# Two z blocks as plain products in place of four, and token sums by DMA

## The chip, the cores and the metric

The kernel runs on one core of a Trainium2 chip. The metric is the device time of one execution in microseconds (us). Each engine has a queue of its own and works it off in order: TensorE (PE) multiplies, VectorE (DVE) and ScalarE (ACT) work elementwise, GpSimd (POOL) here issues DMAs and does a few small operations, SyncE (SP) issues DMAs. An instruction starts when its turn has come and the semaphores that it waits for are there.

## The reference

One layer of a hybrid encoder block on 512 tokens and 16 meta tokens (528 columns), D = 2048:

```python
h = rms_norm(x, norm_g)
proj = h @ w_in                      # 2048 x 12368
(q_a, k_a, v_a, z_a, q_i, k_i, w_i, q_b, f_b, i_b, z_b, gates) = jnp.split(proj, cuts, axis=-1)
...
score = jnp.einsum('bqhs,bqh->bqs', jax.nn.relu(idx_logits), wib)   # token indexer, 16 heads
_, sel = lax.top_k(score, topk)
...
y_b = o_b.reshape(B, T, BRANCH_WIDTH) * jax.nn.silu(z_b)
...
merged = jnp.sum(g * p, axis=2)
return x + merged @ w_out
```

The change concerns `h @ w_in`, and there the columns of `z_b`, which are eight blocks of 128.

## The kernel before

Every fp32 operand is held as a high and a low part (names ending in H and L, or wh and wl for weights), and each product is three matmuls: high by high, high by low, low by high. The token matrix h is kept turned, in 16 row blocks hH[k], hL[k] of 128 x 528 (two halves of 264 columns).

The columns of w_in are computed in two ways. A plain job (`Job`) takes one block of 128 columns: 16 row blocks x 3 matmuls of 512 columns into one PSUM tile pg. A pair (`Pair`, `run_pair`) takes two blocks of 128 columns by a scheme with seven products instead of eight: 7 x 8 x 3 matmuls of 256 columns. The seven are listed in `SEVEN` (L1317): each names a weight operand (`11`, `s2`, `12`, `s3`, `s1`, `22`, `s4`, of which s1 to s4 are sums of weight chunks) and a token operand (`11`, `t2`, `21`, `t3`, `t1`, `t4`, `22`). A weight operand is split by ScalarE (wh) and VectorE (wl) just ahead of its product; three buffers of each stand in turn. The sums s1 and s2 are made on VectorE, s3 and s4 by an adding DMA from GpSimd's queue (L118).

The token operands t1 to t4 are made once, for row blocks k = 0 to 7 with their partners 8 + k, by two tasks of `tops_task` (L1272), which run beside the plain jobs. For one k: r1 = hH[k] + hL[k] and r2 of the partner (two VectorE operations of 528 columns, tiles tr), differences of their halves, and the splits (tiles tT). t3 is kept aside as a float32 tile and put over the right half of hH[k], hL[k] by `place_t3` (L1305), as soon as no plain job needs that half.

Before the change the order is: the key and index blocks (1 + 8 plain jobs), z blocks 0 to 3 as plain jobs (NZ = 4), then 40 pairs, and after them the branch and output products. Beside the plain jobs run the index tasks: for each head pair the queries are turned and split (tiles qst, from qxc), multiplied with the split keys (kkH, kkL) on TensorE into small tiles psc, passed through ScalarE's relu (rl), and added up on VectorE (score). After the last head the search of the 128 largest (`topk_task`) runs on VectorE.

The order of the instructions is set when the program is built. A planner (class `Core`) keeps a clock for each engine with costs that are written in it, and `pump` lets a task add its next instructions when its time has come by these clocks. An instruction that the planner puts early in a queue still waits on the chip for what it reads. Tiles come from 69 equal buffers (`Slots`); a new tile takes the free one whose last use is the oldest by the planner's clocks, and its first writer waits for that last use.

Of the kernel before, what the change touches and what calls it, by code (L numbers as in the profile page):

```python
# [8 lines left out]
F32 = mybir.dt.float32  # L9
F32R = mybir.dt.float32r  # L10
BF16 = mybir.dt.bfloat16
U8 = mybir.dt.uint8
AF = mybir.ActivationFunctionType
OP = mybir.AluOpType
# [16 lines left out]
WAIT = object()  # L31
# [7 lines left out]
ROOM = 2  # L39
SAME = {"pe": 0.0, "act": 60.0, "dve": 125.0, "pool": 60.0}  # L40
MARGIN = 300.0
NSLOT = 69
NZ = 4


class Core:
# [70 lines left out]
    def dma_add(self, out, a):  # L117
        self.nc.gpsimd.dma_start(out, a, accum_op=OP.add)  # L118
        return self.at("pool", 4000.0, [out], [out, a])

    def ts(self, out, a, s1, s2, op0, op1=None):
        if op1 is None:
            self.nc.vector.tensor_scalar(out, a, s1, None, op0=op0)
        else:
            self.nc.vector.tensor_scalar(out, a, s1, s2, op0=op0, op1=op1)
        ins = [a] + [s for s in (s1, s2) if s is not None and not isinstance(s, (int, float))]
        return self.at("dve", 65 + 0.53 * self.n(out), [out], ins)
# [57 lines left out]
def hybrid_kernel(ctx, tc, x, meta, vecs, w_in, rows, w_branch, w_out,  # L185
# [7 lines left out]
    E = Core(nc)  # L193
    S = Slots(E, sp, [f"s{i}" for i in range(NSLOT)], [128, T], None)
# [4 lines left out]
    tasks, hold = [], []  # L199
# [39 lines left out]
    def finish(t):  # L239
        while not t.done:  # L240
            pump(1e9)
            if t.done:
                break
            nxt = [u for u in tasks if u.t > E.clk["pe"]]
            if nxt:
                E.clk["pe"] = max(E.clk["pe"], min(u.t for u in nxt))
            else:
                assert any(u.step() for u in list(tasks)), "stuck"
# [13 lines left out]
    def slots(name, n=1, dt=F32):  # L262
        return [S.get(name, dt) for _ in range(n)]

    def slot(name, dt=F32):
        return S.get(name, dt)
# [238 lines left out]
    hH, hL = [], []  # L505
# [113 lines left out]
    idx_left = [8]  # L619
# [646 lines left out]
    TB = {}  # L1266

    def tops_task(i):


        lo, hi, al = slice(0, 264), slice(264, 528), slice(0, 528)
        for k in range(4 * i, 4 * i + 4):  # L1272
            while len(S.free) < (8 + ROOM if idx_left[0] else 6) or k > 3 and k - 4 not in TB:
                yield WAIT
            if k % 2 == 0:
                t3 = slot("t3")
            r1, r2, t1, c = slots("tr", 4)
            d = t3[:, 264 * (k % 2):264 * (k % 2) + 264]
            E.tt(r1[:, al], hH[k][:, al].bitcast(F32), hL[k][:, al].bitcast(F32), OP.add)
            yield E.tt(r2[:, al], hH[8 + k][:, al].bitcast(F32), hL[8 + k][:, al].bitcast(F32), OP.add)  # L1280
            E.tt(t1[:, lo], r1[:, lo], r1[:, hi], OP.subtract)
            E.tt(t1[:, hi], t1[:, lo], r2[:, hi], OP.add)
            E.tt(d, r1[:, hi], r2[:, hi], OP.subtract)
            e = E.tt(c[:, lo], r2[:, lo], t1[:, hi], OP.subtract)
            S.put(r1, r2)
            yield e
            a, b, t4 = slots("tT", 3, F32R)
            E.act(a[:, al], t1[:, al], AF.Copy)
            E.act(t4[:, lo], c[:, lo], AF.Copy)
            E.tt(b[:, al], t1[:, al], a[:, al].bitcast(F32), OP.subtract)  # L1290
            e = E.tt(t4[:, hi], c[:, lo], t4[:, lo].bitcast(F32), OP.subtract)
            S.put(t1, c)
            TB[k] = {"11": (hH[k][:, lo], hL[k][:, lo]), "t3": (hH[k][:, hi], hL[k][:, hi]),
                     "21": (hH[8 + k][:, lo], hL[8 + k][:, lo]), "22": (hH[8 + k][:, hi], hL[8 + k][:, hi]),
                     "t1": (a[:, lo], b[:, lo]), "t2": (a[:, hi], b[:, hi]), "t4": (t4[:, lo], t4[:, hi]),
                     "tiles": (a, b, t4), "t3f": d, "t3s": t3}
            yield e

    def place_t3(k0):
        for k in range(k0, k0 + 4):  # L1300
            h, l = TB[k]["t3"]
            E.act(h, TB[k]["t3f"], AF.Copy)
            E.tt(l, TB[k]["t3f"], h.bitcast(F32), OP.subtract)
            if k % 2:
                S.put(TB[k]["t3s"])  # L1305
# [13 lines left out]
    def run_pair(pr, nxt, late, last):  # L1319

        w = pr.w
        bk, W, V = {}, slice(0, w), slice(w, 2 * w)
        for i, (wn, tn, bn, on_) in enumerate(SEVEN):
            op = pr.ops[i]
            split_upto(op["prep"] + 2)
            if not on_:
                bk[bn] = B1.get("p" + bn)
            b = bk[bn][:, W]
            for k in range(8):
                th, tl = (t[:, 264 - w:264] for t in TB[k][tn])  # L1330
                st_ = k == 0 and not on_
                E.mm(b, op["h"][k], th, st_, False, loose=True)
                E.mm(b, op["h"][k], tl, False, False, loose=True)
                E.mm(b, op["l"][k], th, False, k == 7, loose=True)
                pump()
            if i == 0:
                p1 = main_slot("p1")
            elif i == 1:
                E.tt(p1[:, V], p1[:, W], b, OP.subtract)
            elif i == 3:  # L1340
                E.tt(p1[:, W], b, p1[:, W], OP.subtract)
                B1.put(bk["y"])
            elif i == 4:
                g2 = main_slot("g2")
                E.tt(g2[:, V], p1[:, W], b, OP.subtract)
            elif i == 5:
                E.tt(g2[:, W], p1[:, W], b, OP.add)
                B1.put(bk["w"])
            elif i == 6:
                E.tt(g1[:, V], p1[:, V], b, OP.add)  # L1350
                B1.put(bk["z"])
                S.put(p1)
            if i == 1:
                sum_4(pr)
            if i > 2 and i < 6 and nxt:
                (sum_1, sum_2, sum_3)[i - 3](nxt)
            split_upto(op["prep"] + 3)
            if i == 0:
                E.act(p1[:, W], b, AF.Copy)
            if late:  # L1360
                late.pop(0)()
            if i == 2:
                g1 = main_slot("g1")
                E.act(g1[:, W], b, pr.f)
                B1.put(bk["x"])
            elif i == 5:
                late.append(lambda g=g2: pr.done[1](g))
            elif i == 6:
                late.append(lambda g=g1: pr.done[0](g))
            if last:  # L1370
                if i == 1:
                    while len(y_out) < 8:
                        pump(1e9)
                        if len(y_out) < 8:
                            E.clk["pe"] += 200
                    yr = load_y(0, 4, nc.scalar)
                elif i == 3:
                    S.put(*hH[:8], *hL[:8])
                    yr += load_y(4, 8, nc.gpsimd)
                    ysplit = split_y(yr, 1)  # L1380
                elif i == 4:
                    S.put(*[t for k in range(8) for t in TB[k]["tiles"][:2]])
                elif i == 5:
                    S.put(*[TB[k]["tiles"][2] for k in range(8)])
                elif i == 6:
                    S.put(*hH[8:], *hL[8:])
                    late.pop(0)()
                    load_gates(1, 0)
                if i in (4, 5):
                    for _ in range(4):  # L1390
                        next(ysplit, None)
# [174 lines left out]
    t_task = []  # L1566

    def pre_t():
        t_task.extend(spawn(tops_task(i), 2) for i in range(2))
# [10 lines left out]
    jobs += [Job("in", C_QI + 128 * j, 128, done=d_qi(j)) for j in range(8)]  # L1580
    jobs += [Job("in", C_ZB + 128 * h, 128, done=d_zb(h)) for h in range(NZ)]
    jobs[3].pre = pre_t
# [15 lines left out]

    for h in range(NZ, 8, 2):
        two(Z[h], Z[h + 1])  # L1600
# [69 lines left out]
    for half in range(2):  # L1670
        n = (272, 256)[half]
        for kt in range(KT):
            prep_next()
            for ji in range(2):
                if ji == 0:
                    c = slice(272 * half, 272 * half + n)
                    o = kb[:80, half, :n]
                else:
                    c = slice(8 + 264 * half, 264 + 264 * half)
# [13 lines left out]
    npair, late, ahead = 0, [], []  # L1693
    first_out = min(i for i, j in enumerate(jobs) if j.kind == "out")
    for ji, job in enumerate(jobs[2:], 3):
# [5 lines left out]
        if job.kind == "pair":  # L1701
            npair += 1
            if npair == 1:
                for t in t_task:
                    finish(t)
                place_t3(0)
                place_t3(4)
                late += [lambda: None, lambda: hold.clear()]
            last = npair == len(pairs)
            run_pair(job, None if last else jobs[ji], late, last)  # L1710
            continue
        if job.kind == "out":
# [4 lines left out]
            nxt = jobs[ji] if ji < len(jobs) else None  # L1717
# [6 lines left out]
        if job.meta:  # L1724
            b = [B1.get("pg"), B1.get("pg")]
            parts = [(b[c][:, :264], slice(264 * c, 264 * c + 264)) for c in range(2)]
        else:
            b = B1.get("pg")
# [104 lines left out]
```

## Time and profile before

| what | us |
|---|---|
| three runs | 1515.77, 1517.16, 1517.38 (median 1517.16) |
| profiled execution, its own time | 1516.59 |
| span of its instructions | 1514.8 |
| TensorE, VectorE, ScalarE, GpSimd busy | 1498.3, 1176.8, 679.3, 199.8 |
| plain jobs | 51.4 to 197.06 |
| last index product ends | 166.14 |
| first pair | 197.06 to 216.91 |

A profile row gives the start, the time and the shape of an instruction or a group; a bracket at its end gives how long the engine had been idle and what ended that. TensorE's granted clock is 1.00 in every stretch. Matmuls overlap, so what one costs is the distance of two starts, not its own time.

### The profile page before, as it was taken

The numbers are of one execution on the slowest core, as the hardware profiler recorded it, in microseconds if no ns is written. First come the engines' busy times: TensorE is split into PE (matmuls) and PEld (weight loads), VectorE is DVE, ScalarE is ACT, GpSimd is POOL, SyncE is SP. The second block draws the span as 40 slices with busy tenths as digits, with TensorE's granted clock in tenths as the row PEclk, the third lists the DMA queues.
The fourth block names the chain that finished last, engine by engine and source line by source line (L and its number), as shares of the span: only waits on it lengthen the run. The fifth ranks groups of instructions, "written<-read, shape, count | busy, mean of one in ns | idle before, by whom it ended". The sixth has DMA issues, their size and how long they took to land.

```text
span 1514.8 us, 30989 instructions
## 1 busy us (share of the span) xinstructions
PE 1498.3 (99%) x12648; PEld 1418.5 (94%) x12648; DVE 1176.8 (78%) x1971; ACT 679.3 (45%) x1048; POOL 199.8 (13%) x241
## 2 busy tenths in 40 slices
PE   7999999999999999999999999999999999999998
PEld 6888899999999999999999999999998888889998
DVE  6699999999998778678868786886665565878775
ACT  5555444444444433443344334434456662334332
POOL 3100000001111100000010000000032110102222
PEclk9999999999999999999999999999999999999999
DMA  9222368776877765675666657666798444548773
GB/s 268 84 70 70 104 147 190 186 182 166 219 200 197 187 156 134 168 168 134 168 162 149 157 138 176 158 143 167 181 271 283 146 132 125 155 136 213 215 213 85
DMA packets 300959, 250.08 MB, mean 165 GB/s; under 512 B 12932, under 2 KB 267920, under 8 KB 300816
## 3 DMA queue, kind: packets, MB, share of 16 engines
q1 hardware_dynamic: 274080, 167.95, 37.9%
q0 software_dynamic: 20656, 72.81, 24.5%
q10 hardware_dynamic: 6080, 7.34, 1.4%
q8 instruction: 99, 1.62, 0.4%
q14 instruction: 44, 0.36, 0.1%
HBM read 168.00 MB, written 27.62 MB: 129 GB/s over the span
## 4 chain that ended last, share of the span: by engine, by line
PE 97%; ACT 1%; issue 1%; DVE 0%; DMA 0%; POOL 0%; ACTq 0%; DVEq 0%; POOLq 0%
PE pg L94 21%; PE pz L92 16%; PE py L92 16%; PE px L92 16%; PE po L92 10%; PE pw L92 8%; PE phl L94 2%; PE psc L94 1%; PE pov L92 1%; PE plg L94 1%; PE pho L94 1%; PE ppt L98 1%; PE phs L94 1%; PE px L98 1%; PE pqa L98 0%
## 5 line engine op out<-in xcount | busy, mean ns | idle before, releaser
L102 ACT ACTIVATE wh<-raw 128x1024 fp32r<-128x1024 f32 x304 | 322.1, 1061 | 509.0 <-PE pz L92 129.4
L109 DVE TENSOR_TENSOR wl<-raw,wh 128x1024 fp32r<-128x1024 f32 x302 | 372.7, 1235 | 133.4 <-ACT wh L102 132.0
L92 PE MATMUL px<-hH,wh 128*128 128x256 f32 (+1 forms) x672 | 193.7, 288 | 0.0
L92 PE MATMUL px<-hH,wl 128*128 128x256 f32 (+1 forms) x672 | 189.5, 282 | 0.0
L92 PE MATMUL px<-hL,wh 128*128 128x256 f32 (+1 forms) x672 | 189.4, 282 | 0.0
L102 ACT ACTIVATE wh<-sum 128x1024 fp32r<-128x1024 f32 x100 | 106.1, 1061 | 180.3 <-PE pw L92 72.5
L92 PE MATMUL po<-wh,mh 128*128 128x256 f32 x896 | 158.6, 280 | 0.5 <-DVE xq L109 0.5
L109 DVE TENSOR_TENSOR wl<-sum,wh 128x1024 fp32r<-128x1024 f32 x100 | 127.1, 1271 | 34.8 <-ACT wh L102 34.6
L92 PEld LDWEIGHTS po<-wh,mh 128*128 128x128 f32 x896 | 137.5, 189 | 0.8 <-DVE xq L109 0.7
L92 PEld LDWEIGHTS px<-hH,wh 128*128 128x128 f32 x672 | 126.6, 188 | 0.9
L92 PEld LDWEIGHTS px<-hH,wl 128*128 128x128 f32 x672 | 126.6, 188 | 0.0
L92 PEld LDWEIGHTS px<-hL,wh 128*128 128x128 f32 x672 | 126.4, 188 | 0.0
L92 PE MATMUL po<-wl,mh 128*128 128x256 f32 x448 | 125.8, 281 | 0.0
L92 PE MATMUL py<-tT,wh 128*128 128x256 f32 (+1 forms) x672 | 124.7, 285 | 0.0
L92 PE MATMUL pw<-tT,wh 128*128 128x256 f32 (+1 forms) x672 | 124.6, 285 | 0.0
L92 PE MATMUL pz<-tT,wh 128*128 128x256 f32 (+1 forms) x672 | 123.6, 284 | 0.0
L118 POOL DMA_DIRECT2D raw<-raw x50 | 43.2, 863 | 518.4 <-DVE sum L109 518.4
L92 PEld LDWEIGHTS py<-tT,wh 128*128 128x128 f32 x672 | 103.4, 189 | 0.5
L92 PEld LDWEIGHTS pw<-tT,wh 128*128 128x128 f32 x672 | 103.2, 189 | 0.2
L92 PEld LDWEIGHTS pz<-tT,wh 128*128 128x128 f32 x672 | 103.2, 188 | 0.2
L94 PE MATMUL pg<-yH,wh 128*128 128x512 f32 x256 | 102.9, 402 | 0.0
L94 PE MATMUL pg<-yL,wh 128*128 128x512 f32 x256 | 100.9, 394 | 0.0
(317 smaller groups left out, 3797.0 us busy)
## 6 DMA issues: line engine op xcount, KB each, us to landing
raw<-in_w_in_dram SPq DMA_DIRECT2D x192, 512.0 KB, 4.6
raw<-raw POOLq DMA_DIRECT2D x50, 512.0 KB, 5.3
raw<-sum POOLq DMA_DIRECT2D x50, 512.0 KB, 5.4
raw<-in_w_branch_dram SPq DMA_DIRECT2D x32, 512.0 KB, 5.2
raw<-in_w_out_dram SPq DMA_DIRECT2D x32, 512.0 KB, 3.9
gd<-g SPq DMA_DIRECT2D x32, 256.0 KB, 5.0
g<-gd POOLq DMA_DIRECT2D x30, 256.0 KB, 3.4
x<-in_x_dram SPq DMA_DIRECT2D x16, 256.0 KB, 5.5
```

Source lines behind the costliest of these rows:

```text
L92: self.nc.tensor.matmul(out, lhsT, rhs, start=start, stop=stop, skip_group_check=True)
L94: self.nc.tensor.matmul(out, lhsT, rhs, start=start, stop=stop)
L98: self.nc.tensor.transpose(out, in_, ident)
L102: self.nc.scalar.activation(out, in_, f, **kw)
L109: self.nc.vector.tensor_tensor(out, a, b, op=op)
L118: self.nc.gpsimd.dma_start(out, a, accum_op=OP.add)
```

## The change

```diff
-NZ = 4
+NZ = 2
...
+    def dma(self, out, a, op=None):
+        if op is None:
+            self.nc.gpsimd.dma_start(out, a)
+        else:
+            self.nc.gpsimd.dma_start(out, a, accum_op=op)
+        t = max([self.clk["pool"]] + [self.wr.get(x.tensor.name, (0.0,))[0] for x in (a, out)])
+        self.clk["pool"] = max(self.clk["pool"], t) + 600.0
+        e = t + 3500.0
...
+        def fetch(k):
+            r = slots("tr", 2)
+            for t, q in zip(r, (k, 8 + k)):
+                E.dma(t[:, al], hH[q][:, al].bitcast(F32))
+            for t, q in zip(r, (k, 8 + k)):
+                e = E.dma(t[:, al], hL[q][:, al].bitcast(F32), OP.add)
+            return r, e
...
-            r1, r2, t1, c = slots("tr", 4)
+            a, b, t4 = slots("tT", 3, F32R)
+            if k % 4 < 3 and len(S.free) >= (6 + ROOM if idx_left[0] else 6):
+                nxt = fetch(k + 1)
             d = t3[:, 264 * (k % 2):264 * (k % 2) + 264]
-            E.tt(r1[:, al], hH[k][:, al].bitcast(F32), hL[k][:, al].bitcast(F32), OP.add)
-            yield E.tt(r2[:, al], hH[8 + k][:, al].bitcast(F32), hL[8 + k][:, al].bitcast(F32), OP.add)
-            E.tt(t1[:, lo], r1[:, lo], r1[:, hi], OP.subtract)
-            E.tt(t1[:, hi], t1[:, lo], r2[:, hi], OP.add)
+            E.tt(r1[:, lo], r1[:, lo], r1[:, hi], OP.subtract)
             E.tt(d, r1[:, hi], r2[:, hi], OP.subtract)
-            e = E.tt(c[:, lo], r2[:, lo], t1[:, hi], OP.subtract)
+            E.tt(r2[:, hi], r1[:, lo], r2[:, hi], OP.add)
+            e = E.tt(r2[:, lo], r2[:, lo], r2[:, hi], OP.subtract)
...
@@ run_pair
+            if i == 1:
+                while t_task:
+                    finish(t_task.pop(0))
             for k in range(8):
-                th, tl = (t[:, 264 - w:264] for t in TB[k][tn])
+                th, tl = (t[:, 264 - w:264] for t in (TB[k][tn] if i else (hH[k], hL[k])))
...
@@ before the first pair
-                for t in t_task:
-                    finish(t)
-                place_t3(0)
-                place_t3(4)
-                late += [lambda: None, lambda: hold.clear()]
+                late += [lambda: None, lambda: (place_t3(0), place_t3(4)), lambda: hold.clear()]
```

Two z blocks go from plain jobs to one more pair (41 pairs). r1 and r2 are made in place: a DMA from GpSimd's queue copies the high part, a second adds the low part, 2 + 2 DMAs for each k, 32 in all; the next k is fetched while one is worked on, if buffers are free. The differences are written over r1 and r2, so two tiles fewer are held, and the split of 528 columns becomes two of 264. The first pair begins with its first product while the last row blocks' token operands are still to be made; they are finished in the build order ahead of the second product, and t3 is placed behind the second.

GpSimd's queue had, before, nothing between the key norm and the first adding DMA of a pair; rows of its order there, with the semaphores that each row waits for:

```order
L573 MEMSET kiy_829 128x320 [waits PE_49]
L113 TENSOR_TENSOR kis_830<-kis_830,mhalf 128x5 [waits DVE_49,PE_49]
L118 DMA raw_1840<-raw_1789 128x1024 [waits DMAHW2_49,DMAHW3_49,DMAHW1_49,DMAHW4_49,DVE_49,DMAHW6_49,Activation_49,Pool_49]
L118 DMA raw_2016<-sum_26_2155 128x1024 [waits DMAHW5_49,DMAHW0_49,DMAHW6_49,DVE_49,Pool_49]
L118 DMA raw_2107<-raw_2065 128x1024 [waits DMAHW6_49,DMAHW0_49,DVE_49]
```

Now the 32 DMAs stand between; here those of row block 3 (tr_1355 and its partner tr_1356; hH_361 is hH[3], hH_503 is hH[11]) with the two ahead of them:

```order
L125 DMA tr_1086<-hL_347 128x528 [waits DMASW6_49,DMASW0_49]
L125 DMA tr_1087<-hL_488 128x528 [waits DMASW7_49,DMASW1_49]
L123 DMA tr_1355<-hH_361 128x528 [waits DMASW1_49,DVE_49]
L123 DMA tr_1356<-hH_503 128x528 [waits DVE_49]
L125 DMA tr_1355<-hL_362 128x528 [waits DMASW4_49,DMASW2_49]
L125 DMA tr_1356<-hL_504 128x528 [waits DMASW5_49,DMASW3_49]
```

The copies wait for VectorE (the former user of the buffer), the adds for the copies, and the first adding DMA of a pair now stands behind all of them, right after the last row block's (7):

```order
L125 DMA tr_2019<-hL_556 128x528 [waits DMASW5_49,DMASW3_49]
L123 DMA tr_2028<-hH_438 128x528 [waits PE_49]
L123 DMA tr_2029<-hH_569 128x528 [waits DMAHW4_49,DMAHW0_49,DVE_49]
L125 DMA tr_2028<-hL_439 128x528 [waits DMASW6_49,DMASW0_49]
L125 DMA tr_2029<-hL_570 128x528 [waits DMASW7_49,DMASW1_49]
L118 DMA raw_1626<-raw_1540 128x1024 [waits DMAHW5_49,DMAHW2_49,DMAHW6_49,DMAHW0_49,Pool_49]
```

Row block 7's partner tile waits for VectorE too. On VectorE, between the last tT of row block 2 (tT_1231, which reads the buffer that tr_1355 takes) and the first operation on tr_1355 stands:

```order
L109 TENSOR_TENSOR tT_1231<-tr_1087,tT_1231 128x264
L145 SCALAR_TENSOR_TENSOR score_975<-rl_1293,tabs_98,score_975 128x272
L109 TENSOR_TENSOR tT_1098<-tr_1045,tT_1097 128x264
L109 TENSOR_TENSOR tT_1098<-tr_1046,tT_1097 128x264
L109 TENSOR_TENSOR tT_1099<-tr_1046,tT_1099 128x264
L109 TENSOR_TENSOR wl_1306<-raw_858,wh_1305 128x1024
L145 SCALAR_TENSOR_TENSOR score_976<-rl_1320,tabs_98,score_976 128x400
L109 TENSOR_TENSOR qst_1328<-qxc_1261,qst_1328 64x512
L109 TENSOR_TENSOR qst_1329<-qxc_1261,qst_1329 64x512
L145 SCALAR_TENSOR_TENSOR score_977<-rl_1340,tabs_98,score_977 128x528
L145 SCALAR_TENSOR_TENSOR score_974<-rl_1349,tabs_98,score_974 128x144
L109 TENSOR_TENSOR tr_1355<-tr_1355 128x264
```

Before, a row block's sums stood in VectorE's queue themselves and could not be late for it; the like stretch there:

```order
L109 TENSOR_TENSOR tT_1263<-tr_1108,tT_1262 128x528
L109 TENSOR_TENSOR tT_1264<-tr_1109,tT_1264 128x264
L109 TENSOR_TENSOR wl_1273<-raw_858,wh_1272 128x1024
L130 SCALAR_TENSOR_TENSOR score_983<-rl_1287,tabs_98,score_983 128x400
L109 TENSOR_TENSOR tT_1296<-tr_1046,tT_1295 128x528
L109 TENSOR_TENSOR tT_1297<-tr_1047,tT_1297 128x264
L130 SCALAR_TENSOR_TENSOR score_984<-rl_1305,tabs_98,score_984 128x528
L130 SCALAR_TENSOR_TENSOR score_981<-rl_1314,tabs_98,score_981 128x144
L109 TENSOR_TENSOR qst_1320<-qxc_1239,qst_1320 64x512
L109 TENSOR_TENSOR qst_1321<-qxc_1239,qst_1321 64x512
L130 SCALAR_TENSOR_TENSOR score_982<-rl_1332,tabs_98,score_982 128x272
L109 TENSOR_TENSOR tr_1339<-hH_346,hL_347 128x528
```

The third place is TensorE's queue at the first index products (psc_985 before, psc_978 now), in the third plain job; a piece of the difference:

```order
+L94 MATMUL psc_978<-kkH_962,qst_875 128x144
+L94 MATMUL psc_978<-kkL_963,qst_875 128x144
 L94 MATMUL pg_904<-hH_503,wh_854 128x512
 L94 MATMUL pg_904<-hL_504,wh_854 128x512
 L94 MATMUL pg_904<-hH_503,wl_855 128x512
+L94 MATMUL psc_1007<-kkH_962,qst_875 128x272
+L94 MATMUL psc_1007<-kkL_963,qst_875 128x272
 L94 MATMUL pg_904<-hH_522,wh_854 128x512
 L94 MATMUL pg_904<-hL_523,wh_854 128x512
 L94 MATMUL pg_904<-hH_522,wl_855 128x512
-L94 MATMUL psc_985<-kkH_969,qst_875 128x144
-L94 MATMUL psc_985<-kkL_970,qst_875 128x144
```

The first index product moved ahead of six plain ones.

More of the change, by code (lines that the diff above doesn't have):

```diff
@@ L119, in dma_add @@
         return self.at("pool", 4000.0, [out], [out, a])
+    def dma(self, out, a, op=None):
[6 more added lines that the diff above has]
+        e = t + 3500.0
+        for x in (a, out):
+            w = self.ac.get(x.tensor.name)
+            if not w or w[0] < e:
+                self.ac[x.tensor.name] = (e, "dma")
+        self.wr[out.tensor.name] = (e, "dma")
+        return e
     def ts(self, out, a, s1, s2, op0, op1=None):
@@ L1271, in tops_task @@
         lo, hi, al = slice(0, 264), slice(264, 528), slice(0, 528)
-        for k in range(4 * i, 4 * i + 4):
-            while len(S.free) < (8 + ROOM if idx_left[0] else 6) or k > 3 and k - 4 not in TB:
+        def fetch(k):
[5 more added lines that the diff above has]
+            return r, e
+        nxt = None
+        for k in range(4 * i, 4 * i + 4):
+            while k > 3 and k - 4 not in TB:
+                yield WAIT
+            while not nxt and len(S.free) < (6 + ROOM if idx_left[0] else 6):
+                yield WAIT
+            (r1, r2), e = nxt or fetch(k)
+            nxt = None
+            yield e
+            while len(S.free) < (4 + ROOM if idx_left[0] else 4):
                 yield WAIT
@@ L1276, in tops_task @@
                 t3 = slot("t3")
-            r1, r2, t1, c = slots("tr", 4)
+            a, b, t4 = slots("tT", 3, F32R)
+            if k % 4 < 3 and len(S.free) >= (6 + ROOM if idx_left[0] else 6):
+                nxt = fetch(k + 1)
             d = t3[:, 264 * (k % 2):264 * (k % 2) + 264]
-            E.tt(r1[:, al], hH[k][:, al].bitcast(F32), hL[k][:, al].bitcast(F32), OP.add)
-            yield E.tt(r2[:, al], hH[8 + k][:, al].bitcast(F32), hL[8 + k][:, al].bitcast(F32), OP.add)
-            E.tt(t1[:, lo], r1[:, lo], r1[:, hi], OP.subtract)
-            E.tt(t1[:, hi], t1[:, lo], r2[:, hi], OP.add)
+            E.tt(r1[:, lo], r1[:, lo], r1[:, hi], OP.subtract)
             E.tt(d, r1[:, hi], r2[:, hi], OP.subtract)
-            e = E.tt(c[:, lo], r2[:, lo], t1[:, hi], OP.subtract)
-            S.put(r1, r2)
[L1286 to L1292, printed above, removed]
+            E.tt(r2[:, hi], r1[:, lo], r2[:, hi], OP.add)
+            e = E.tt(r2[:, lo], r2[:, lo], r2[:, hi], OP.subtract)
+            yield e
+            E.act(a[:, lo], r1[:, lo], AF.Copy)
+            E.act(a[:, hi], r2[:, hi], AF.Copy)
+            E.act(t4[:, lo], r2[:, lo], AF.Copy)
+            E.tt(b[:, lo], r1[:, lo], a[:, lo].bitcast(F32), OP.subtract)
+            E.tt(b[:, hi], r2[:, hi], a[:, hi].bitcast(F32), OP.subtract)
+            e = E.tt(t4[:, hi], r2[:, lo], t4[:, lo].bitcast(F32), OP.subtract)
+            S.put(r1, r2)
             TB[k] = {"11": (hH[k][:, lo], hL[k][:, lo]), "t3": (hH[k][:, hi], hL[k][:, hi]),
```

## The prediction

> **What bounds the kernel now.** I read the page first (busy shares, then the chain that ended last), then the waits of TensorE over the whole span, then that chain in order of time where the edits stand.
>
> ```profile
> span 1514.8 us, 30989 instructions
> PE 97%; ACT 1%; issue 1%; DVE 0%; DMA 0%; POOL 0%; ACTq 0%; DVEq 0%; POOLq 0%
> PE pc L98 <- DMA vrow<-in_vecs_dram: 8.2, 1, 8.2
> PE phl L98 <- ACT wh L102: 1.1, 1, 1.1
> PE phs L94 <- ACT MT L102: 1.0, 5, 0.2
> PE pg L94 <- POOL el L113: 0.8, 1, 0.8
> ```
>
> TensorE carries 97% of the chain. It waits 8.2 us once at the start and then hardly at all: the largest later wait is 1.1 us. So only two things move the end: how long TensorE's own work is, and every microsecond for which it is newly made to wait.
>
> ```profile
> 166.14 30.91 PE pg L94 x132
> 197.06 2.85 PE px L92 x24
> ...
> 214.09 2.83 PE pz L92 x24
> 216.91 2.84 PE px L92 x24
> 80.00:100.00 20.00, 20.00 (x100) 16.88 (x99) 19.77 (x39) 10.81 (x21) 0.00 (x0) 1.00 0.29 80
> ```
>
> At 166.14 the last index product is over and 132 plain products run without a gap; the first pair takes 197.06 to 216.91. The last row is a stretch of the plain jobs in the windows view: the fourth busy figure says VectorE is busy for 19.77 of 20 us (and GpSimd for 0). VectorE is nearly full beside a TensorE that doesn't yet wait for it.
>
> **The change, part by part. Plain blocks.** A plain product costs 30.91 / 132 = 0.234 us, and a block has 48: two blocks are 96 x 0.234 = 22.48 us. In their place stands one pair more, 216.91 - 197.06 = 19.85 us. TensorE's own work falls by **2.63 us**. That is the ceiling of the gain: nothing else on TensorE gets shorter. The split of four weight chunks on ScalarE and VectorE goes and seven operands' splits and two sums come; they lie beside the extra pair as in every pair now. The order of TensorE's last 6976 rows, some two thirds, is unchanged, so I add nothing for the later phases.
>
> A rule stands against the row here. The Trainium skill, "TensorE: Matmul & The Clock Gate", section "Back-to-back issue gap", gives a gap of N / 2.4 + 2.5 ns; by it the products take 215.8 and 109.2 ns and the gain would be 2.37 us. The trace has 234 and 118 ns at a granted clock of 1.00, so it doesn't agree, and the rows decide.
>
> **First index product.** The eight row blocks' two 528-wide sums leave VectorE.
>
> ```profile
> 69.25 1.32 DVE L109 TENSOR_TENSOR tr<-hH,hL 128x528 f32<-128x528 f32 x2
> 70.49 1.22 DVE L109 TENSOR_TENSOR wl<-raw,wh 128x1024 fp32r<-128x1024 f32 x1
> 71.63 0.43 DVE L109 TENSOR_TENSOR kkL<-pki,kkH 128x272 fp32r<-128x272 f32 x1
> 72.51 0.42 DVE L109 TENSOR_TENSOR kkL<-pki,kkH 128x256 fp32r<-128x256 f32 x1 [0.45 <-ACT kkH L102]
> 68.62 1.06 ACT L102 ACTIVATE wh<-raw 128x1024 fp32r<-128x1024 f32 x1 [3.10 <-PE pg L94]
> 72.09 0.39 ACT L102 ACTIVATE kkH<-pki 128x256 fp32r<-128x256 f32 x1 [2.10 <-DVE kkL L109]
> 72.89 0.23 PE L94 MATMUL psc<-kkH,qst 128*128 128x144 f32 x1
> 72.96 0.27 PE L94 MATMUL psc<-kkL,qst 128*128 128x144 f32 x1
> ```
>
> A pair of sums takes 70.49 - 69.25 = 1.24 us. The planner therefore puts the first index product six plain products (6 x 0.234 = 1.4 us) earlier, at 71.49. But kkL comes only 0.7 us earlier: wl is held by its wh on ScalarE until 69.7 (68.62 + 1.06), so wl runs 69.7 to 70.9, the first kkL to 71.3, kkH (0.39) to 71.7, the second kkL (0.42) to 72.2. The kkL product, due at 71.56, waits until 72.2. Stall **0.6 us**; bounds 0 (if the planner's order happens to fit) and 1.4 (kkL no earlier than now).
>
> **Fetches.** Each row block now needs two copies and two adding DMAs from GpSimd's queue, 32 in all.
>
> ```profile
> L118 POOL DMA_DIRECT2D raw<-raw x50: 842/854/934, 189.3 to 1483.2; - x50
> DMA to landing us min/median/max: 4.5/5.4/8.0
> DMA to landing us min/median/max: 2.2/3.5/15.8
> g<-gd POOLq DMA_DIRECT2D x30, 256.0 KB, 3.4
> kv<-kd POOLq DMA_DIRECT2D x8, 264.0 KB, 7.2
> ```
>
> GpSimd is idle here, so 32 x 0.85 us of issuing costs nothing; what counts is latency. No 264 KB add is in the trace. A plain transfer of that size has 3.4 (g) to 7.2 us (kv, in a crowded stretch); an add of twice the size has 4.5 to 8.0, median 5.4. I take 3.4 for the copy and 4.2 for the add, nearest to the quiet rows: 7.6 us from the release of the buffer to the landed sum, some 0.8 more if both halves are late; ends 6.5 (2.2, the fastest among the transfers of g, and 4.3) and 13 (5.8 and 7.2). The planner counts 3.5 for each of the two and doesn't look at when the buffer is free. Most fetches are early. Two are not.
>
> Row block 3 (tr_1355) gets the buffer that the fetch before leaves after its last tT. Between that and its first use VectorE has this work:
>
> ```profile
> 100.14 1.04 DVE L109 TENSOR_TENSOR tT<-tr,tT 128x528 fp32r<-128x528 f32 x2
> 102.79 1.04 DVE L109 TENSOR_TENSOR tT<-tr,tT 128x528 fp32r<-128x528 f32 x2
> 106.68 0.70 DVE L109 TENSOR_TENSOR tr<-hH,hL 128x528 f32<-128x528 f32 x1
> 115.86 1.41 DVE L109 TENSOR_TENSOR qst<-qxc,qst 64x512 fp32r<-64x512 f32 x2
> 118.22 0.23 PE L94 MATMUL psc<-kkH,qst 128*128 128x144 f32 x1
> ```
>
> The stretch 100.14 to 106.68 has the same operations with one tT pair (0.96 us) more, so 5.6 us. VectorE then stands for 8.4 - 5.6 = 2.8 us, and what is queued behind is two weight splits, scores and the next head's qst. In before that qst half is done at 116.6 and TensorE takes it at 118.22: 1.6 us of slack, 2.3 with the first stall. Stall **0.5 us**; bounds 0 (landed within 7.9 us of the release) and 5 (fetch 13). Row block 5 waits in the same way, but its head's products come some 6 us after, so it is covered.
>
> **First pair.** It begins where the plain work ends, at 166.14 + 36 x 0.234 = 174.57 (before: 197.06, less the two blocks), with row block 7 and t3 missing.
>
> ```profile
> 163.32 0.69 DVE L109 TENSOR_TENSOR hz<-pg,hz 128x512 f32<-128x512 f32 x1 [1.27 <-ACT hz L102]
> 198.33 2.83 DVE L109 TENSOR_TENSOR hL<-t,hH 128x264 fp32r<-128x264 f32 x8
> ```
>
> The last fetch waits for VectorE's score of 272 columns. From hz at 163.3 come hz (0.6), two sums and a split (3 x 1.2) and that score (0.4): 167.9. Sum landed: 167.9 + 7.6 + 0.1 = 175.6; VectorE would reach it at 173.2. After it: three 264-wide operations (0.35 each, 2.83 / 8), hz 0.6, wl 1.14, two tT: 179.1. TensorE reaches that operand, the last eighth of the second product, at 174.57 + 2.84 + 2.48 = 179.9: 0.8 us to spare. The eight t3 pieces follow the second product's end (180.25): ScalarE's 1.06, wl 1.14, then 0.35 each, last at 185.4; needed from 183.1 to 185.6: 0.2 us to spare. So no wait by the sum, and each later microsecond is one of waiting. I take **0.3 us**; bounds 0 and 5.
>
> Sum: -2.63 + 0.6 + 0.5 + 0.3 = **-1.2 us**. The profiled execution took 1516.59 us (span 1514.8 and 1.8 around it); the median shown is 1517.16, 0.6 higher, runs 1515.77 to 1517.38. Prediction **1515.4 us**. A difference of 0.2%, 3.0 us, is about what a measurement can tell from no change; the ceiling of the gain is 2.63, so it is "no change" unless a stall goes wrong.
>
> The Trainium skill, "DMA: Bandwidth & Descriptors", section "Anatomy of one DMA — SWDGE (gpsimd) path", gives 2.0 us plus bytes / 436 GB/s: 2.6 us for each transfer here and 5.2 for a fetch. By that rule both fetch stalls vanish (a rival below). For the 512 KB add it would give 3.2, where the rows have 5.4: the trace doesn't agree, and I don't use it.
>
> **Rivals.** *Clean*: fetches and kkL are on time, the full 2.63 us: 1514.0. For it: no row of TensorE shows a wait now though VectorE is as full. Against: the kkL arithmetic.
> *Fetches in time*: at the low end, 6.5 us, row block 3 is held for 6.5 + 0.8 - 5.6 = 1.7 us, inside its slack, and the first pair gains a microsecond; kkL alone remains: -2.63 + 0.6, 1514.6. Against: 2.2 us is the fastest of 30 rows.
> *Cancelled*: each stall is 1 us larger: -2.63 + 4.4, 1518.4. For it: slacks of 0.2 and 0.8 us.
> *Slower: fetch latency takes over the first pair and row block 3.* If copies and adds land like the crowded rows (5.8 and 7.2, 13 us in all, 5.4 later than I take), TensorE waits 5.4 + 0.5 at row block 3 and some 5 at the first pair: -2.63 + 0.6 + 11 = +9, 1525.6. It turns slower than before from a fetch of about 9 us, by 0.2% from some 10.5. Against: DMA share is 0.29 in the plain stretch. A mechanism that would do it: VectorE keeping GpSimd from issuing. The rows speak against that: all 50 issues took 842 to 934 ns beside a busy VectorE.
> That starving is what the Trainium skill describes in "SBUF — State Buffer", section "SBUF: two separate sides", for VectorE's 2-port modes; the trace doesn't show it, and I give it 0.02 of this rival's chance.
> *The change doesn't do what it says*: the count of products in the built order agrees (96 plain ones fewer, 168 half-width ones more), so I give it nothing.
>
> **Chances.** Forecast 0.40, clean 0.12, fetches in time 0.14, cancelled 0.17, slow fetches 0.17. Half of clean and a third of fetches in time may read as faster by over 0.2%, since the runs scatter by 1.6 us: 0.11. Slow fetches nearly all read slower: 0.16. The rest, 0.73, is within 0.2%. Range: clean less the scatter of the runs, 1513.7, to past the cancelled case, 1519.8; half the slow case and little else lies outside.
>
> **What would show it.** In the profile after: 1200 instead of 1296 plain products of 512 columns and a first pair from about 176; TensorE's waits list a psc product waiting for VectorE's kkL (0.6 us) near 72; GpSimd's DMA tr rows with 3 to 4.5 us to landing; VectorE idle before tr for a DMA twice (2 to 3 us); waits in the first pair under 1 us. I am wrong if TensorE waits in sum over 3 us there, if fetches take over 10 us, or if later waits differ by over 1 us.

## The result, and the profile after

| kernel | median us | runs | ratio to before, 95% interval |
|---|---|---|---|
| before | 1516.68 | 1515.48 to 1517.38 | |
| after | 1524.59 | 1523.93 to 1526.37 | 1.0053 [1.0043, 1.0064] |

The change makes the kernel slower by some 8 us; predicted was no change. The span went from 1514.8 to 1522.9. The page of the kernel after, span and chain that ended last:

```profile
span 1522.9 us, 31221 instructions
PE 88%; DVE 4%; issue 3%; DMA 2%; ACT 1%; POOL 1%; ACTq 0%; POOLq 0%; DVEq 0%
```

TensorE had 97% of the chain; now 9% has gone to VectorE, issue and DMA. Some stretch must have been ruled by them. TensorE's waits (us in total, times, longest), those that were not there before:

```profile
PE psc L94 <- ACT rl L102: 4.2, 1, 4.2
PE pz L92 <- DVE g L109: 1.4, 2, 0.7
PE psc L94 <- DVE qst L109: 0.5, 2, 0.3
PE py L92 <- DVE p L109: 0.3, 1, 0.3
```

That is 6.4 us, and not one of them is in the first pair. The chain in order of time (start, us, what), where the plain jobs end:

```profile
173.83 8.42 PE pg L94 x36
182.25 2.85 PE px L92 x24
185.10 2.83 PE py L92 x24
...
202.13 2.84 PE px L92 x24
```

The first pair runs without a gap, 202.13 - 182.25 = 19.88 us; but it begins at 182.25 and not at 174.57, and the last index product ends at 173.83 and not at 166.14. So 7.7 us were lost before it, nearly all among the index products (0.4 at the very start). VectorE's waits for DMAs there, from 52 to 182 us:

```profile
DVE tr L109 <- DMA tr<-hL: 4.5, 3, 2.9
DVE t L109 <- DMA tr<-hL: 3.9, 3, 1.9
```

VectorE stood for 8.4 us before sums that had not landed: near 83 (row block 4, 2.1 us), near 113 (row block 3, 3.7) and near 152 (row block 5, 2.7). The middle one, in the chain (tr<-hH are copies, tr<-hL adds):

```profile
103.71 0.46 POOL tr L123
...
107.29 5.89 DMA tr<-hL
...
117.30 0.58 DVE qxc L109
...
117.99 0.62 ACT rl L102
...
118.65 1.07 PE psc L94 x4
119.72 2.56 PE pg L94 x6
```

The copies were issued from 103.71 on, the second add landed at 107.29 + 5.89 = 113.18: 9.5 us. The engines' timelines show how that reaches TensorE (VectorE's rows, ScalarE's, TensorE's):

```profile
108.00 1.05 DVE L145 SCALAR_TENSOR_TENSOR score<-rl,tabs,score 128x528 f32<-128x528 f32 x2
111.98 0.43 DVE L109 TENSOR_TENSOR tr<-tr 128x264 f32<-128x264 f32 x1 [2.94 <-DMA tr<-hL]
113.20 0.43 DVE L109 TENSOR_TENSOR t<-tr,tr 128x264 f32<-128x264 f32 x1 [0.78 <-DMA tr<-hL]
...
117.20 0.67 DVE L109 TENSOR_TENSOR qxc<-xqi,cq 128x512 f32<-128x512 f32 x1
```

```profile
117.99 0.79 ACT L102 ACTIVATE rl<-psc 128x528 f32<-128x528 f32 x2 [7.06 <-DVE qxc L109]
```

```profile
118.65 0.41 PE L94 MATMUL psc<-kkH,qst 128*128 128x264 f32 x1 [4.21 <-ACT rl L102]
```

A few operations behind the sum in VectorE's queue stands qxc, the next head pair's turning of the queries. It is the last reader of xqi (the queries before they are turned). The next rl reads nothing of qxc, so what it waits for is a buffer that qxc sets free: the planner gave it that of xqi. So ScalarE's rl waits 7.06 us for VectorE, its psc is not emptied, and TensorE, which wants a place in PSUM (the memory that it writes to) for the next psc, waits 4.21 us. Then something more, in the windows view (start and end of the stretch, its length, busy time of TensorE, weight loads, VectorE, ScalarE and GpSimd, then TensorE's granted clock):

```profile
114.00:118.00 4.00, 0.44 (x2) 0.00 (x0) 3.96 (x9) 0.01 (x1) 0.00 (x0) 1.00 0.16 32
118.00:120.00 2.00, 1.35 (x6) 1.25 (x7) 1.97 (x4) 2.00 (x7) 0.00 (x0) 0.72 0.66 199
120.00:122.00 2.00, 2.00 (x6) 1.60 (x5) 2.00 (x6) 1.98 (x5) 0.00 (x0) 0.50 0.01 4
122.00:124.00 2.00, 2.00 (x11) 1.69 (x10) 1.97 (x3) 1.68 (x4) 0.00 (x0) 0.93 0.04 9
```

After the wait the granted clock is 0.50. The six plain products at 119.72 take 2.56 us in place of 6 x 0.234 = 1.40, the four psc products 1.07 in place of about 0.5 (the pieces of that shape took 0.12 each elsewhere): 1.7 us more, which no list of waits shows. The clock gives the same: 2 x (0.28 + 0.50 + 0.07) = 1.7 us less than full from 118 to 124.

From the distances of the starts in both traces: from 52 to 100 us the kernel after loses 0.8 us more than before, from 110 to 130 5.9 (4.2 of waiting, 1.7 of low clock), from 160 to 170 0.6: 7.3 by the first pair. The pairs from 400 to 500 lose another 2.2. With -2.63 that is +6.9; the last 1.2 are 0.4 at the very start (the first load's wait is 8.6 in place of 8.2) and small differences over the last 980 us. The same stretch, on TensorE in the same order, took 972.5 to 973.7 us in the profiled executions of before and of the kernels below (h3800_s4 alone took over a microsecond more), so this last part is not put down to the change.

### The profile page after: what moved, and what is told of

It is laid out like the page before. It is cut to its first block, busy times and chain, and to the rows that moved or that the text cites. A ratio compares the mean times of both kernels' runs of the same rounds, so it can differ in the third digit from the quotient of the medians.

```text
span 1522.9 us, 31221 instructions
## 1 busy us (share of the span) xinstructions
PE 1499.9 (98%) x12720; PEld 1422.1 (93%) x12720; DVE 1175.1 (77%) x1973; ACT 684.1 (45%) x1061; POOL 225.6 (15%) x275
## 3 DMA queue, kind: packets, MB, share of 16 engines
q10 hardware_dynamic: 6080, 7.34, 1.4%
## 4 chain that ended last, share of the span: by engine, by line
PE 88%; DVE 4%; issue 3%; DMA 2%; ACT 1%; POOL 1%; ACTq 0%; POOLq 0%; DVEq 0%
PE pz L92 16%; PE py L92 15%; PE px L92 15%; PE pg L94 15%; PE po L92 10%; PE pw L92 8%; PE phl L94 2%; PE pov L92 1%; PE plg L94 1%; PE pho L94 1%; DMA tr<-hL 1%; PE ppt L98 1%; ACT wh L102 1%; DVE wl L109 1%; DVE score L145 1%
## 5 line engine op out<-in xcount | busy, mean ns | idle before, releaser
L92 PE MATMUL px<-hH,wh 128*128 128x256 f32 (+1 forms) x688 | 198.0, 288 | 0.0
L92 PE MATMUL px<-hH,wl 128*128 128x256 f32 (+1 forms) x688 | 193.7, 282 | 0.0
L92 PE MATMUL px<-hL,wh 128*128 128x256 f32 (+1 forms) x688 | 193.7, 282 | 0.0
L92 PE MATMUL py<-tT,wh 128*128 128x256 f32 (+1 forms) x688 | 128.2, 285 | 0.0
L92 PE MATMUL pz<-tT,wh 128*128 128x256 f32 (+1 forms) x688 | 126.9, 284 | 0.0
L94 PE MATMUL pg<-yH,wl 128*128 128x512 f32 x256 | 100.9, 394 | 0.0
```

Of the source, the lines that this page charges most:

```text
L92: self.nc.tensor.matmul(out, lhsT, rhs, start=start, stop=stop, skip_group_check=True)
L94: self.nc.tensor.matmul(out, lhsT, rhs, start=start, stop=stop)
```

## Experiments

Two theories at first. **Hold**: VectorE, in order, stands before sums that have not landed, and what is behind it is late. **Room**: 22.5 us less of plain work is too short a stage for VectorE's work, whoever makes the sums. After the first four runs a third, **margin**, for the pairs near 400: a transfer that lands just in time in the kernel before lands too late now. All ratios are to the kernel before, whose median was 1516.85 to 1516.98 in these groups.

### honest: a fetch counts from the release of its buffer

```diff
-        t = max([self.clk["pool"]] + [self.wr.get(x.tensor.name, (0.0,))[0] for x in (a, out)])
+        t = max([self.clk["pool"]] + [self.wr.get(x.tensor.name, (0.0,))[0] for x in (a, out)]
+                + [self.ac.get(out.tensor.name, (0.0,))[0]])
```

> The changed kernel; only the planner's estimate of a fetch now counts from when the buffer is released, so that VectorE's operations on the sum are put later in its queue. Theory 'hold': VectorE's waits for a DMA in the plain stage fall from 8.4 to under 4 us, the 4.2 us wait of TensorE near 114 goes with the low clock behind it, index products end at 167 to 170, time 1516 to 1520. Theory 'room': the place in the queue is of no account, time 1522.5 to 1526.

1518.59 us, 1.0012 [1.0003, 1.0021]. Of VectorE's operations on the sums, those on row block 3 stand 10 rows later and the others in the rows where they were. VectorE's waits for DMAs, and the first pair in the chain:

```profile
DVE t L109 <- DMA tr<-hL: 1.2, 1, 1.2
DVE tr L109 <- DMA tr<-hL: 0.9, 1, 0.9
```

```profile
166.55 9.12 PE pg L94 x39
175.66 2.85 PE px L92 x24
```

What is left is row block 4's wait. TensorE's wait of 4.2 us and the low clock behind it are gone, the first pair begins 6.6 us earlier, and six of the eight microseconds are back, with all 32 transfers still there. As "hold" said; "room" expected no effect.

### copy_only: the same order, a shorter fetch

```diff
-            self.nc.gpsimd.dma_start(out, a, accum_op=op)
+            pass
```

> The changed kernel without the 16 adding DMAs of the fetches (the token sums then lack the low parts); the planner counts them as before, so that the order on TensorE, VectorE, ScalarE and SyncE is row for row that of the change. Only the time from the release of a buffer to the landed tile falls, from 9.5 to about 4 us for row block 3. Theory 'hold': VectorE's waits for DMAs in the plain stage go from 8.4 to under 1 us, index products end at 165.9 to 166.8, the first pair starts at 174.6 to 175.5, and what is left is what the pairs lose later (0 to 2.2 us): 1514.5 to 1518. Rival 'place' (VectorE's new order is bad by itself, without a late transfer): index products end at 170 or later, 1520 or more.

This kernel leaves out the 16 adds, so its token sums lack the low parts. 1516.00 us, 0.9994 [0.9984, 1.0005]. VectorE's list of waits in the plain stage has no DMA any more, and the chain has

```profile
165.88 8.42 PE pg L94 x36
174.30 2.85 PE px L92 x24
```

The first pair begins 8 us earlier than in the change, 0.3 before the 174.57 of the prediction. This is the clearest run: TensorE, VectorE, ScalarE and SyncE have the same order, and only the transfers have changed: 16 fewer, and each sum there earlier. The place in the queue does no harm by itself; a transfer that is later than that place does.

### dma_only: the sums by DMA and nothing else

```diff
-NZ = 2
+NZ = 4
...
+                for t in t_task:
+                    finish(t)
+                place_t3(0)
+                place_t3(4)
-                late += [lambda: None, lambda: (place_t3(0), place_t3(4)), lambda: hold.clear()]
+                late += [lambda: None, lambda: hold.clear()]
```

> The kernel before with nothing changed but the token sums: four plain z blocks, first pair begins when all operands are there, sums by copying and adding DMAs. Theory 'hold': the same waits of VectorE for a sum come (some 8 us in all) and index products end 5 to 8 us later than in before; part of it may be met by the two z blocks that follow only if TensorE's own order has them behind, which it has not, so the time is 1520 to 1525. Theory 'room': VectorE has 9.9 us less to do and the stage is as long as before, so no loss: 1515.5 to 1517.5.

1525.81 us, 1.0060 [1.0047, 1.0073], a little above the upper end (the profiled execution was the longest of five, 1529.74). The stage is as long as before and VectorE has less to do, and yet index products end near 176 in place of 166. "Room" alone is out. Two waits of TensorE for rl this time, the first of 2.09 us ending at 91.6; and already that one is followed by the low clock:

```profile
89.00:91.50 2.50, 0.48 (x3) 0.04 (x1) 2.47 (x6) 2.50 (x7) 0.00 (x0) 1.00 0.98 177
...
93.50:95.50 2.00, 2.00 (x6) 1.61 (x5) 2.00 (x3) 0.88 (x3) 0.00 (x0) 0.50 0.11 19
```

### sums_dve: the sums back on VectorE

The body of `tops_task` is the one of before; two plain z blocks and the early first pair stay.

```diff
-            (r1, r2), e = nxt or fetch(k)
...
+            r1, r2, t1, c = slots("tr", 4)
+            E.tt(r1[:, al], hH[k][:, al].bitcast(F32), hL[k][:, al].bitcast(F32), OP.add)
+            yield E.tt(r2[:, al], hH[8 + k][:, al].bitcast(F32), hL[8 + k][:, al].bitcast(F32), OP.add)
```

> The changed kernel with the token sums back on VectorE (two 528-wide additions for each row block, as before); two plain z blocks and the early first pair stay. Theory 'hold' (VectorE, in order, stands before a sum that has not landed, and the index chain behind it is late; 7.3 us at TensorE): the waits for a DMA go, index products end at 166 to 167.5 in place of 173.8, first pair from 174.6 to 176. VectorE has 16 x 0.62 = 9.9 us more to do, so a wait of 0 to 4 us may come in the first pair; time 1514 to 1518.5. Theory 'room' (the stage shortened by 22.5 us is too short for VectorE's work, whoever makes the sums): VectorE's work grows by 9.9 us, index products end at 174 or later, time 1524 or more.

1525.59 us, 1.0054 [1.0040, 1.0067]: the time that "room" gave ("hold" had 1514 to 1518.5), by a way that neither theory had whole. The first pair begins at 175.5, as "hold" said, since no sum is late. Then its second product waits for the last operands:

```profile
PE py L92 <- ACT tT L102: 4.4, 2, 2.6
PE py L92 <- DVE tT L109: 0.5, 2, 0.4
```

4.9 us with the clock at 0.50 from 186 to 192 behind them. "Room" is right to this extent: with two plain blocks VectorE, in this order, doesn't get the sums done in time, and the DMAs can (honest_s4 below).

### rash: sums used earlier

```diff
-        e = t + 3500.0
+        e = t + 2750.0
```

> The changed kernel with the planner counting 2.75 us in place of 3.5 for each DMA of a fetch, so that VectorE's operations on the sums stand some 5 to 15 rows earlier in its queue (row blocks 0, 1, 4 and 2) and the transfers are the same. Theory 'hold': VectorE waits longer for DMAs than the 8.4 us of the change, 10 to 16 us, index products end 2 to 7 us later than 173.8, time 1526 to 1532. Theory 'room' (the amount of work decides, not its place): 1523 to 1526 as with the change.

1524.58 us, 1.0043 [1.0030, 1.0056]: a miss for "hold", and the time that "room" named. VectorE waits 8.8 us for DMAs, hardly more than 8.4, and index products end at 175.3. But the waits moved with the place of the sums, of which "room" knows nothing: one of 5.2 us of TensorE for rl near 90, none near 114. A hold early on makes all later uses later too, and their transfers are then in time; holds don't add up row by row.

### honest5: more time allowed for a fetch

```diff
-        e = t + 3500.0
+        e = t + 5000.0
```

(with the edit of honest)

> As honest (a fetch counts from the release of its buffer), and 5.0 us in place of 3.5 for each of its DMAs: the operations on the sums of row blocks 4 and 5 go 14 and 18 rows later in VectorE's queue. Theory 'hold': the 2.1 us that VectorE still waits for DMAs in honest go to under 1 us, index products end at 165.5 to 166.5, the first pair starts at 174.6 to 175.3, at most 1 us under honest: 1516.5 to 1518.5. Against it: row blocks 6 and 7 come later too and may make the first pair wait 1 to 3 us.

1522.62 us, 1.0036 [1.0024, 1.0048]. VectorE waits for no DMA, but index products end about 3 us later than in honest, and the first pair waits 3.4 us for the last row blocks' operands: the risk that was named decided. Some 1.4 of the 3 us lie ahead of the first index product: in this profile the granted clock is 0.63 from 18 to 22 us, where honest has 1.00. The profiles of sums_dve, rash and before_s4 have such a stretch too, so it isn't put down to the edit. Why the rest is later was not followed up.

### early_only, and what it found

Four plain z blocks, sums on VectorE, and of the change only the early first pair:

```diff
...
+            if i == 1:
+                while t_task:
+                    finish(t_task.pop(0))
...
-                for t in t_task:
-                    finish(t)
-                place_t3(0)
-                place_t3(4)
-                late += [lambda: None, lambda: hold.clear()]
+                late += [lambda: None, lambda: (place_t3(0), place_t3(4)), lambda: hold.clear()]
```

> The kernel before with the early first pair alone: four plain z blocks, sums on VectorE; the last operands finished ahead of the second product and t3 placed behind it. Both theories: VectorE has the whole plain stage, the operands are there long before, waits under 0.5 us in the first pair: 1516 to 1517.5, no change. A rival, that the late t3 costs by itself, would show waits of 1 to 3 us in the first pair.

1519.62 us, 1.0016 [1.0007, 1.0024]: slower by 2.7 us, which no theory had. The first pair has no wait. TensorE waits 2.0 us for g in the pairs near 355 and 400, at the place where the kernel after waits near 404. The chain of early_only before the second of these:

```profile
387.55 0.49 POOL kay L113
...
388.55 8.42 DMA raw<-sum
...
397.07 1.07 ACT wh L102
...
400.05 0.34 DVE g L109
```

The adding DMA that makes the sum s4 stands in GpSimd's queue behind the power of the key norm (kay), which waits for VectorE. It lands 8.42 us after its issue, and VectorE's g stands behind the split of what it brings. In the kernel before the same DMA was issued at 387.96, its wh started at 395.02, and g was ready 0.3 us ahead of its product (397.92 + 0.41 against 398.63):

```profile
397.92 0.41 DVE L109 TENSOR_TENSOR g<-p,pz 128x256 f32<-128x256 f32 x1
```

```profile
398.63 0.28 PE L92 MATMUL pz<-hH,wh 128*128 128x256 f32 x1
```

### after_s4, early_s4 and before_s4: the adding DMA ahead of the power

```diff
             if i == 1:
+                sum_4(pr)
                 while t_task:
                     finish(t_task.pop(0))
...
-            if i == 1:
-                sum_4(pr)
```

> The changed kernel, with the adding DMA for s4 issued ahead of the second product's matmuls in the build order in place of behind them: in GpSimd's queue it then stands ahead of the key norm's power and no longer waits for VectorE's kay. Theory 'margin' (the 2.2 us lost in the pairs from 400 to 500 come from this DMA, which lands 0.4 us before it is needed in the kernel before and later than needed after the change): the waits of TensorE for g and p there (1.7 us with their gaps 2.5) go, the plain stage is unchanged (first pair at 181.5 to 183), time 1522 to 1523.5. Rival 'full' (VectorE, 95% busy there, is late by itself): waits as with the change, 1524 to 1526.

1522.27 us, 1.0031 [1.0020, 1.0042], 2.3 us below the kernel after. GpSimd's rows show the new order, the DMA five microseconds earlier:

```profile
388.04 0.84 POOL L118 DMA_DIRECT2D raw<-sum  x1 [8.88 <-DVE wl L109]
392.53 1.03 POOL L113 TENSOR_TENSOR kay<-kay,mhalf 128x4 f32<-128x4 f32 x1 [3.65 <-DVE kay L140]
```

Both waits for g are gone, the plain stage is as in the change (first pair at 182.6).

> The kernel before with the early first pair (as early_only) and the adding DMA for s4 ahead of the second product. Theory 'margin': the waits of early_only for g and p from 355 to 413 (2.3 us) go, 1516.3 to 1517.8. Rival 'full': as early_only, 1519 to 1520.

1516.47 us, 0.9991 [0.9982, 1.0000]: the 2.7 us of early_only are back. The early first pair by itself costs nothing.

> The kernel before with nothing changed but the adding DMA for s4, ahead of the second product. Theory 'margin': the DMA lands in time in the kernel before, so nothing is gained: 1516 to 1517.5. Rival: the edit is a gain in any kernel, of some 2 us: 1514.5 to 1515.5.

1516.32 us, 0.9995 [0.9985, 1.0005]: no gain where the DMA had landed in time. "Margin" holds in all three.

### honest_s4 and h3800_s4: the change with its two faults taken away

> Both edits: a fetch counts from the release of its buffer, and the adding DMA for s4 ahead of the second product. Theory 'hold' with 'margin': what honest still loses in the pairs near 397 and 410 (two waits, 1.1 us with their gaps) goes: 1516.5 to 1517.8. Rival 'full': as honest, 1518 to 1519.5.

1516.49 us, 0.9995 [0.9986, 1.0003]: at the lower end of the range named, and the same as before by what a measurement can tell.

> As honest_s4, with 3.8 us in place of 3.5 for each DMA of a fetch; the planner then fetches row block 5 ahead of row block 3 into a buffer that comes free earlier, and puts the operations on row block 4 14 rows later. Theory 'hold': VectorE's waits for DMAs under 1.5 us (2.4 in honest_s4), no index product waits, the first pair starts at 174.6 to 175.1: 1515.3 to 1516.5. Against it: row block 7 comes some rows later and the first pair may wait 1 to 3 us for it: 1517.5 to 1519.5.

1520.14 us, 1.0017 [1.0007, 1.0027]. The first pair begins as early as in copy_only, within 0.1 us, and then waits 2.2 us for the last operands: what was named against it. The time is 0.6 us above what was named for that; the granted clock is 0.50 again from 184 to 186. No version was found that beats both kernels by more than the interval; the ceiling of 2.63 us is 0.17%.

## Why the prediction was wrong

**Plain blocks, -2.63: right.** In copy_only, where no sum is late, the first pair begins 197.06 - 174.30 = 22.76 us earlier than in before (0.25 of that from the first load, which TensorE waits for 8.0 in place of 8.2 us), and in the kernel after it takes 19.88.

**First index product, 0.6: mis-sized.** The product's rows have no bracket, so no wait; the lower bound, 0, was the value:

```profile
71.83 0.23 PE L94 MATMUL psc<-kkH,qst 128*128 128x144 f32 x1
71.90 0.27 PE L94 MATMUL psc<-kkL,qst 128*128 128x144 f32 x1
71.18 0.43 DVE L109 TENSOR_TENSOR kkL<-pki,kkH 128x272 fp32r<-128x272 f32 x1
72.06 0.42 DVE L109 TENSOR_TENSOR kkL<-pki,kkH 128x256 fp32r<-128x256 f32 x1 [0.45 <-ACT kkH L102]
```

My reckoning of kkL held: its second piece is done at 72.48, where I said 72.2. But the product at 71.90 reads 144 columns, which lie in the first piece of 272, done at 71.61, and it runs before the second piece exists. I had made it wait for both.

**"Most fetches are early. Two are not": wrong by one.** The third fetch (row block 4) was late too. The first four fetches follow one another on GpSimd (copies issued from 59.5, 66.0, 72.3 and 79.8 us), and I had looked only at the two whose buffers come free late. VectorE stood 2.1 us; 0.8 us were lost at TensorE.

**Row block 3, 0.5: the step that failed.** The hold was priced nearly right: 9.5 us of fetch where I said 8.4, VectorE held 3.7 us where I said 2.8. What failed was the slack of "2.3 with the first stall". I read it off the qst product alone. The path that decides goes another way: sum, qxc behind it in VectorE's queue, xqi's buffer, rl on ScalarE, the PSUM bank, TensorE. There was no slack on it, and nothing behind absorbed the lag, since VectorE is busy for 19.77 of 20 us (before, 80 to 100). Measured 4.2 us of waiting; and the half clock behind it, 1.7 us, was in no term of the sum. The upper bound of 5 was passed by the two together.

**Row block 5 "covered": wrong.** VectorE stood 2.7 us, and at 164.61 TensorE, some 10 us on, waits for qst; 0.6 us are lost there. How much of that is this hold and how much the lag of the earlier ones was not taken apart; in honest, where the last copy of this fetch is issued at 132 in place of 145, neither the hold nor the loss is there.

**First pair, 0.3: not contradicted, and not tested.** TensorE has no wait in it in the kernel after, nor in honest, where it begins 6.6 us earlier. But even there it begins 1.1 us later than the 174.57 of the sum, more than the 0.8 us that the last row block had to spare; where it begins at 174.3, the fetches are shorter (copy_only) or VectorE's order is another (h3800_s4).

**"I add nothing for the later phases": failed.** The reason that I gave holds for TensorE's last rows alone. In the traces its order is the same from 502 us on in before and 509 in after; the 2.2 us were lost ahead of that, from 400 to 500. There VectorE's and ScalarE's operations are placed anew by the planner's clocks, some small products of TensorE (pka, pkm) too, and what hangs on one DMA had 0.3 us to spare. That cost the 2.2 us; after_s4 and early_s4 show that this DMA is the cause. In early_only it is issued 0.6 us later than in before and takes 1.4 us longer; why it takes longer stays open. I had taken the order of one engine, in part of the span, for the order of all engines in the rest of it.

The rival "slow fetches" had the right sign and row block 3 as a place, but its size, +9, was luck: it came from a fetch of 13 us, with half of the loss in the first pair. The fetch took 9.5, the first pair lost nothing, and by its own way of reckoning 9.5 in place of 8.4 gives some +1 us. The copies and adds of the fetches took a median of 4.0 us from issue to landing, up to 6.1:

```profile
L123 POOL DMA_DIRECT2D tr<-hH x16: 546/580/1078, 59.5 to 176.4; - x16
L125 POOL DMA_DIRECT2D tr<-hL x16: 859/889/1128, 62.5 to 179.3; - x16
...
DMA to landing us min/median/max: 2.3/4.0/6.1
```

The prediction's estimate of 2.6 us for each, by the fit in the Trainium skill, "DMA: Bandwidth & Descriptors", section "Anatomy of one DMA — SWDGE (gpsimd) path", is not borne out by these rows; by it, both fetch stalls would have vanished.

## What to carry to other kernels

Work that is moved from an in-order engine to a DMA can become a wait at the place where its result is used: that place has to be reckoned from the release of the buffer plus the measured latency, and ten rows later in the queue was worth 6 us here. To price such a wait, follow everything that stands behind it, buffers that it frees included, to the bound engine, and not only the nearest consumer. And where the order of several engines comes from one planner, an edit early on shifts transfers everywhere: list the margins under a microsecond, on every queue, before writing a zero for the rest.

## What the hardware showed that was not expected

A wait of TensorE can cost more than its length. After 4.2 us of waiting the granted clock was 0.50 and back near 1 some 4 us later; after 2.1 us in dma_only it was 0.50 too; in the kernel before, without such waits, it is 1.00 throughout the plain jobs. Not every wait does it: after the 1.6 us for g near 400 in early_only it stayed at 1.00. The Trainium skill, "TensorE: Matmul & The Clock Gate", section "Part 1: The HAM clock gate", has the half clock and says that it comes after at least one idle window of about 3.4 us. The trace agrees on the half; the 2.1 us of dma_only is shorter than that window.

The adding DMAs vary more than their margins: the one for s4 took 8.42 us from issue to landing in early_only and about 7.0 in before (387.96 to 395.0), with honest and copy_only between them (7.39 and 7.34).
